# Weight combinations of the down projection: all twelve on GpSimd in the mix stage, tokens loaded earlier, one sample product moved

## The chip, the cores and the metric

The kernel runs on one core of a Trainium2 chip. TensorE (PE) multiplies, VectorE (DVE) and ScalarE (ACT) work on tiles, GpSimd (POOL) does too, SyncE (SP) only issues DMAs; DMAs are issued from the queues of SP, ACT and POOL and run on the same 16 DMA engines. The metric is the time of one execution on the device in microseconds, as the median of the runs shown; lower is better.

## The reference

One step of a decoder layer for 512 prompt tokens and 64 sample tokens (8 sequences of 8). Everything up to the merge of the two attention branches is untouched by the change. What follows it:

```python
br_fox = einsum('btk,kd->btd', o_fox, w_br_fox)      # 512 -> 1024
br_nsa = einsum('btk,kd->btd', o_nsa, w_br_nsa)      # 512 -> 1024
mix = g_fox * br_fox + g_nsa * br_nsa                # gates: sigmoid of 2 x 1024 columns of h @ w_in
x = x + gt1 * einsum('btd,de->bte', mix, w_out)      # 1024 -> 1024
h = rms_norm(x, norm2_g) * (1 + sc2) + sh2
u = relu(einsum('btd,df->btf', h, w_up))             # 1024 -> 4096
y = x + gt2 * einsum('btf,fd->btd', u * u, w_down)   # 4096 -> 1024
```

## The kernel before

A float32 product is made of three passes over halves: each operand is split into a high part (`split`, line 130: an ACT copy, the profile's L113) and a rest (a DVE subtraction, L132), and PE multiplies high by high, low by high and high by low (L78). So every weight tile takes a DMA into a raw tile, an ACT and a DVE instruction before PE can use it. Three raw tiles of 512 KB (`praw`, tag raw) and one more (`pn3`) are shared by all loads of the late stages: a load waits until the split of the tile's last user is done.

The order on each engine is set when the program is built: a scheduler simulates the program and emits each engine's instructions in the order that it finds; a `pin` or `issue_after` keeps an instruction behind a named one in that order. On the chip each engine and each DMA queue takes its instructions strictly in that order.

Four stages matter here.

- **Mix** (`mix_part`). For each of eight column blocks e: two gate products (mg) and two branch products (br) on PE, each with its weights split just before. Beside it POOL makes weight combinations for the down projection. `w_down` is used in a Strassen-like scheme for its rows 0 to 3071: seven products over half matrices in place of eight. Three of these (T1, T2, T3) and T4 need differences of the blocks of w_down. For each k of 0 to 11, two 128-row pieces (one of the upper, one of the lower 1536 rows) are loaded into two tiles td, four subtractions are made in place (`down_sums`), and both tiles are stored to DRAM (tD), from which the late products load them. In the kernel before POOL makes k = 0 to 7 here, with three td tiles, so the loads of the next k wait for a store of the last one.
- **Out** (`out_part`): w_out in four quarters wo0 to wo3. The tiles for wo3's halves lie where the td tiles lay, so wo3's split on ACT waits until the last td store has landed.
- **Up** (`mlp_up`). Pairs n = 3 to 15 of 256 columns, each seven products of 12 matmuls (upNa, upNb, upNe). DVE adds the products from PSUM into a tile u (L101); there are two u tiles. ACT squares u and stores it to DRAM (sD), three DMAs per pair. POOL makes the sums of w_up that a pair needs (L2176). In the kernel before, after pairs 5 and 8 SP loads k = 8, 9 and k = 10, 11 of w_down, 1 MB in each of two DMAs; DVE makes their differences (L1970) in the next iteration, each instruction twice as wide as POOL's; POOL stores them. At the end of the stage `u_load` (in iterations 11, 12, 13) fetches the first two token chunks of sD and splits them (as), and the sample tokens' first block.
- **Down** (`mlp_down`). Products p = 0 to 6 ("11", "21", "T3", ...), each over three chunks c of 512 rows: 24 matmuls dn per chunk on the 256 tokens of a half, with the chunk's weights (wd, 4 places in turn) and tokens (as). For products 0, 1, 4 and 5, each chunk also has a sample part: 8 matmuls dns with sample tokens (sa, or as for the first). In the kernel before, the sample part of chunk c stands right behind chunk c's dn matmuls.

Of the kernel before, what the change touches and what calls it, by code (L numbers as in the profile page):

```python
# [6 lines left out]
F32 = mybir.dt.float32  # L7
# [4 lines left out]
OP = mybir.AluOpType  # L12
AX = mybir.AxisListType

P = 128
D = 1024
# [3 lines left out]
NS = 64  # L20
NT = SEQ + NS
HALF = NT // 2
SQ = 3
# [23 lines left out]
class Step:  # L47
# [1830 lines left out]
    def mix_part(self, pq, pr, mix2):  # L1878
# [49 lines left out]
        def weights(e, x):  # L1928
# [2 lines left out]
                    self.stream(pq, br_src(x, e), [P, 4, P], "wb", f"{x}_{e}", raws=0, parts=1, pin=pin,  # L1931
                                after=None if e else self.first))

        for e in range(NK):
            if e == 0:
                ws = [weights(0, x) for x in range(2)]
                for k in range(8):
                    self.split(oH[:, k], oL[:, k], self.oT[:, k])
                m = [gate(e, x, ws[x][0], True) for x in range(2)]
                for x in range(2):  # L1940
                    branch(e, x, ws[x][1], m[x])
            else:
                m = []
                for x in range(2):
                    mg, br = weights(e, x)
                    m.append(gate(e, x, mg))
                    branch(e, x, br, m[x])
            if e == NK - 1:
                self.wo0 = self.out_weights(0)
            nc.vector.tensor_tensor(m[0], m[0], m[1], op=OP.add)  # L1950
            self.split_pack(mix2[:, e], m[0])
            for k in ((), (0,), (1,), (2, 3), (4,), (5, 6), (7,), ())[e]:
                b = [pq.tile([P, 1, D], F32, tag="td", bufs=3, name=f"td{k}_{i}") for i in range(2)]
                with self.tc.issue_after(self.last_mm):
                    self.down_rows(b, k, "gpsimd")
                    self.down_sums(b, nc.gpsimd)
                    self.down_store(b, k)

    def down_rows(self, b, k, eng):

        n = b[0].shape[1]
        for i in range(2):
            r0 = SQ * 512 * i + P * k
            self.dma(eng, b[i], self.I["w_down"][0, r0:r0 + n * P, :].rearrange("(k p) c -> p k c", p=P))

    def down_sums(self, b, eng):

        (b11, b12), (b21, b22) = [[t[:, :, 512 * h:512 * h + 512] for h in range(2)] for t in b]
        for out, x, y in ((b11, b12, b11), (b12, b22, b12), (b22, b22, b11), (b21, b22, b21)):
            eng.tensor_tensor(out, x, y, op=OP.subtract)  # L1970

    def down_store(self, b, k):

        n = b[0].shape[1]
        for i in range(2):
            self.dma("gpsimd", self.tD[k // 2][:, k % 2:k % 2 + n, i], b[i])

    def gate_prompt(self, pool, j0, scale, uid, **kw):

# [125 lines left out]
        t = pool.tile([P, 4, 2 * NT], F32R, tag=tag, bufs=1, name=f"u2{blk}")  # L2105
        return [t[:, q] for q in range(4)]

    def token_part(self, pool, half, blk, uid, eng="gpsimd", tag="u"):

        t = pool.tile([P, 4, 256], F32, tag=tag, bufs=3, name=f"a{uid}")  # L2110
# [9 lines left out]

    def sample_part(self, pool, tag, blks, room):

        x = pool.tile([P, 4 * len(blks), NS], F32, tag=tag, bufs=3 if tag == "raw" else 1, name=f"sr{blks[0]}_{self.turn}")
# [64 lines left out]
    def mlp_up(self, pu, h3):  # L2188
# [27 lines left out]
        for n in range(FIRST, NP + 1):  # L2216
# [12 lines left out]
                self.tt(o[0][1], b, x, OP.add)  # L2229
            if left:  # L2230
                left()
            if n in (5, 8):
                kd = 8 if n == 5 else 10
                td = self.pb.tile([P, 2, 2, D], F32, tag="x", bufs=1, name=f"td{kd}")
                td = [td[:, i] for i in range(2)]
                self.down_rows(td, kd, "sync")
            if n in (6, 9):
                with self.pinned((self.splits[-1],)):
                    self.down_sums(td, self.nc.vector)
            if n in (7, 10):  # L2240
                self.down_store(td, kd)
            if 0 <= n - NP + 5 < 3:
                self.u_load(n - NP + 5)
            if n == NP:
                break
            product(E, s1, t1, True)
# [6 lines left out]
            def left(n=n, w22=w22, s4=s4, B=B, E=E, b=b, e=e, x=x, u=u, o=o):  # L2253
# [4 lines left out]
                self.act(u, u, AF.Relu)  # L2258
                self.squares_out(n, u)
        self.chain = None  # L2260

    def mlp_down(self, pf):
        nc, I, O = self.nc, self.I, self.O
# [8 lines left out]
        def chunk(key, c):  # L2272

            def src(s):
                if key[0] == "T":
                    v = self.tD[2 * c + s.start // 2][:, :, key in ("T2", "T4")]
                    h = key in ("T2", "T3")
                else:
                    r0, h = 512 * (c + SQ * (key[0] == "2")) + P * s.start, key[1] == "2"
                    v = W[r0:r0 + 256].rearrange("(k p) c -> p k c", p=P)  # L2280
                return [((slice(None),), v[:, :, 512 * h:512 * h + 512])]

            return self.stream(None, src, [P, 4, 512], "wd", f"{key}_{c}", raws=0, room=room(f"wd{key}_{c}", 4))
# [4 lines left out]
        a11 = self.keep.tile([P, SQ, 4, 256], F32, tag="r2", bufs=1, name="a11")  # L2288
        left = [pf.tile([P, 4, 256], F32, tag="late", bufs=3, name=f"s2{c}") for c in range(SQ)]

        def tokens(p, c):

            part = lambda half, blk: self.token_part(pf, half, blk, f"{p}_{half}{blk}")
            if p == 0:
                return part(0, c)
            if p == 1:
                self.dma("gpsimd", a11[:, c], self.sD[c][:, 0:1024].rearrange("p (k t) -> p k t", k=4))
                return part(0, SQ + c)
            if p == 2:
                x, y = part(1, c), part(1, SQ + c)  # L2300
                self.tt(x, a11[:, c], x, sub)
# [13 lines left out]
        sb = None  # L2315
        for p, key in enumerate(("11", "21", "T3", "T2", "T1", "22", "T4")):
# [4 lines left out]
            if sample is not None:  # L2321
                blks = tuple(range(SQ * sample + (p == 0), SQ * sample + SQ))
                xs = self.sample_part(pf, "us", blks, self.ph.tile([P, 4 * len(blks), P], F32R, tag="h3", bufs=2, name=f"sa{p}"))
                xs = xs if p else self.first_sample + xs
            for c in range(SQ):
                w = chunk(key, c)
                if p == 0 and c < 2:
                    a = self.first_parts[c]
                else:
# [2 lines left out]
                for m in range(2):  # L2332
                    n = 0
                    for k in range(4):
                        for x, y in three([t[:, k, P * m:P * m + P] for t in a], [t[:, k] for t in w]):
                            self.mm(pbs[m], x, y, c + n == 0, c == SQ - 1 and n == 11)
                            n += 1
                if sample is not None:
                    for k in range(4):
                        for e in range(2):  # L2340
                            self.mm(sb, xs[c][:, k], w[e][:, k], c + k + e == 0 and p != 5, c == SQ - 1 and k + e == 4 and p != 4)
            for m, pb in enumerate(pbs):
                if p in (0, 2):
                    self.act((c12 if p == 0 else c21)[m], pb)
# [74 lines left out]
    def run(self):  # L2419
        nc, I, O, keep = self.nc, self.I, self.O, self.keep  # L2420
        self.modT = keep.tile([P, 48, 9], F32, name="modT")
        self.gate = keep.tile([P, 5, 24], F32, name="gate")
        self.logf = keep.tile([P, 5, 8], F32, name="logf")
# [4 lines left out]
        self.vc = op.tile([P, NB, P], F32, name="vc")  # L2428
        self.adw = keep.tile([P, 5 * D], F32, tag="r2", bufs=1, name="adw")
        hf = self.adw[:, 0:NK * NT].rearrange("p (k t) -> p k t", k=NK)  # L2430

# [176 lines left out]
```

## Time and profile before

| | us |
|---|---|
| three runs, median (lowest, highest) | 1193.18 (1192.88, 1194.2) |
| the profiled execution's own time | 1192.07 |
| its span, first to last instruction | 1190.4 |
| PE busy in it | 1142.7 |
| DVE, ACT, POOL busy in it | 807.7, 582.4, 249.8 |
| mean granted TensorE clock | 0.991 |

The stages lie in the span at about 586 to 735 (mix), 736 to 790 (out), 790 to 987 (up, the pairs from 830) and 987 to 1190 (down). Rows of the profile name engine, line, operation and tile (output<-inputs, buffer numbers left out); a bracket at a row's end is the idle time just ahead of it on that engine and what ended it. The chain of waits names for each stretch of time what was late there.

### The profile page before, as it was taken

What the parts mean: (1) busy time and instruction counts of PE and PEld (TensorE: products, weight loads), DVE (VectorE), ACT (ScalarE), POOL (GpSimd) and SP (SyncE); (2) the same over time, 40 slices, a digit from 0 to 9 for tenths busy, and PEclk for the clock granted to TensorE, in tenths of its full rate; (3) what the DMA queues carried; (4) which work ended last, traced back from release to release, by engine and by line L of the source; (5) the groups of instructions that cost most, each with busy time, mean ns of one, the idle gap of its engine ahead of it and who ended that gap; (6) DMA issues with size and microseconds to landing.
All of it is one profiled execution on the core that took longest, in us unless ns stands there. A gap on an engine that the chain in (4) does not pass through costs nothing.

```text
span 1190.4 us, 24438 instructions
## 1 busy us (share of the span) xinstructions
PE 1142.7 (96%) x9051; PEld 979.5 (82%) x9051; DVE 807.7 (68%) x1960; ACT 582.4 (49%) x1176; POOL 249.8 (21%) x291
## 2 busy tenths in 40 slices
PE   4999999999999999999999999999997998999998
PEld 3887789999666656777899999889997997888887
DVE  3688785585888856666654444669676754797686
ACT  2455453444776864545532333366544565554520
POOL 2303100000311130000455540003464422110100
PEclk9999999999999999999999999999999999999999
DMA  9897456795785348899998764355755638977632
GB/s 217 206 253 239 154 149 210 251 314 199 228 278 166 108 168 272 294 315 327 229 290 235 231 204 140 109 176 157 240 190 199 225 118 260 332 232 252 215 123 80
DMA packets 187961, 255.46 MB, mean 215 GB/s; under 512 B 22937, under 2 KB 145506, under 8 KB 185666
## 3 DMA queue, kind: packets, MB, share of 16 engines
q1 hardware_dynamic: 148034, 177.22, 48.0%
q0 software_dynamic: 19696, 62.13, 16.2%
q10 hardware_dynamic: 20112, 14.55, 4.4%
q8 instruction: 71, 1.16, 0.4%
q14 instruction: 48, 0.39, 0.1%
HBM read 217.64 MB, written 57.12 MB: 231 GB/s over the span
## 4 chain that ended last, share of the span: by engine, by line
PE 77%; DVE 7%; DMA 7%; ACT 4%; issue 2%; SPq 1%; POOL 1%; ACTq 0%; DVEq 0%; POOLq 0%
PE dn L78 13%; PE mg L78 9%; PE hid L78 7%; PE z L78 6%; PE br L78 4%; PE wo L78 4%; PE up L78 3%; PE ss L78 2%; PE ct L84 2%; PE dns L78 2%; PE so L78 2%; PE k L84 2%; DMA sD<-u 2%; PE ada L78 2%; PE sp L84 1%
## 5 line engine op out<-in xcount | busy, mean ns | idle before, releaser
L78 PE MATMUL z<-winh,h 128*128 128x264 f32 (+1 forms) x576 | 111.1, 286 | 0.3
L78 PEld LDWEIGHTS z<-winh,h 128*128 128x128 f32 x576 | 91.7, 190 | 2.2 <-DVE h L800 0.9
L78 PE MATMUL z<-winl,h 128*128 128x264 f32 (+1 forms) x320 | 88.2, 284 | 0.5 <-DVE winl L132 0.5
L78 PE MATMUL mg<-hH,wml 128*128 128x288 f32 x256 | 75.3, 296 | 0.9 <-DVE wml L132 0.9
L78 PE MATMUL mg<-hH,wmh 128*128 128x288 f32 x256 | 75.3, 296 | 0.0
L113 ACT ACTIVATE xh<-ct 128x256 fp32r<-128x256 f32 x128 | 48.1, 385 | 55.1 <-PE ct L84 30.0
L78 PE MATMUL mg<-hL,wmh 128*128 128x288 f32 x256 | 72.6, 294 | 0.0
L132 DVE TENSOR_TENSOR xl<-ct,xh 128x256 fp32r<-128x256 f32 x128 | 51.7, 420 | 15.1 <-ACT xh L113 13.3
L78 PEld LDWEIGHTS z<-winl,h 128*128 128x128 f32 x320 | 60.6, 190 | 0.7 <-DVE winl L132 0.7
L132 DVE TENSOR_TENSOR wml<-wmr,wmh 128x1024 fp32r<-128x1024 f32 x14 | 19.9, 1419 | 51.2 <-ACT wmh L113 51.2
L78 PEld LDWEIGHTS mg<-hH,wml 128*128 128x128 f32 x256 | 48.1, 188 | 1.1 <-DVE wml L132 1.1
L78 PEld LDWEIGHTS mg<-hH,wmh 128*128 128x128 f32 x256 | 48.1, 188 | 0.2
L78 PEld LDWEIGHTS mg<-hL,wmh 128*128 128x128 f32 x256 | 47.2, 188 | 0.1
L78 PE MATMUL hid<-xh,w1hlk 128*128 128x512 f32 (+1 forms) x160 | 45.1, 370 | 1.5 <-ACT xh L113 1.5
L78 PE MATMUL hid<-xh,w1hlv 128*128 128x512 f32 (+1 forms) x160 | 44.8, 367 | 0.5 <-ACT xh L113 0.5
L132 DVE TENSOR_TENSOR wp<-sums,wp 128x1024 fp32r<-128x1024 f32 x26 | 38.0, 1469 | 7.2 <-ACT wp L113 6.8
L84 PE MATMUL ct<-identF,ro 128*128 128x128 f32 x256 | 36.4, 281 | 5.9 <-DVE ro L116 5.5
L113 ACT ACTIVATE mgt<-mg 128x288 f32<-128x288 f32 x32 | 12.8, 409 | 57.2 <-PE mg L78 57.2
L132 DVE TENSOR_TENSOR wp<-pu,wp 128x512 fp32r<-128x512 f32 (+1 forms) x26 | 30.6, 1181 | 14.8 <-ACT wp L113 14.8
L113 ACT ACTIVATE u<-u 128x1152 f32<-128x1152 f32 x29 | 33.6, 1159 | 10.4 <-DVE u L101 10.1
L78 PE MATMUL br<-oH,wbh 128*128 128x288 f32 x128 | 37.8, 296 | 0.2 <-ACT mgt L113 0.2
L78 PE MATMUL br<-oH,wbl 128*128 128x288 f32 x128 | 37.7, 295 | 0.0
(1181 smaller groups left out, 3709.0 us busy)
## 6 DMA issues: line engine op xcount, KB each, us to landing
adw<-in_w_ada SPq DMA_DIRECT2D x16, 1024.0 KB
foxD<-in_cache_fox_kv SPq DMA_DIRECT2D x128, 128.0 KB
fr<-foxD SPq DMA_DIRECT2D x28, 512.0 KB
sr<-in_cache_nsa_kv SPq DMA_DIRECT2D x112, 128.0 KB
cpg<-in_cache_nsa_kv SPq DMA_DIRECT2D x104, 128.0 KB
pu<-in_w_up SPq DMA_DIRECT2D x26, 512.0 KB
wdr<-in_w_down SPq DMA_DIRECT2D x26, 512.0 KB
wdrT<-tD SPq DMA_DIRECT2D x24, 512.0 KB
```

The lines of the kernel that those rows point to most:

```text
L78: ins = self.nc.tensor.matmul(out, a, b, start=start, stop=stop, skip_group_check=True)
L84: ins = self.nc.tensor.transpose(out, in_, self.identF[:n, :n])
L113: return self.nc.scalar.activation(out, in_, f, **kw)
L132: self.splits.append((eng or self.nc.vector).tensor_tensor(l, x, h.bitcast(F32), op=OP.subtract).ins)
```

## The change

It has five parts.

1. All twelve k are made by POOL in the mix, two per block e from e = 1 on, with four td tiles (two k at a time). The loads of a k stand ahead of the sums of the k before it. To make room, two small tiles (gate, logf) move from one pool to another, which shifts later addresses by 640 bytes.
2. With that, the SP loads, the DVE subtractions and the POOL stores of k = 8 to 11 leave the up stage.
3. `u_load` runs one iteration earlier (10, 11, 12; a fourth call does nothing).
4. The third token chunk of product 0 (`self.third`) is loaded at the end of the up stage into the pn3 tile, and the first one of product 1 (`second`) ahead of the down stage's other token loads; a pin keeps the split of weight chunk ("21", 1) behind the token splits that stand ahead of it.
5. In product 0 the sample parts of chunks 1 and 2 are written behind chunk 2's dn matmuls.

```diff
+        rows = []
         for e in range(NK):
...
-            for k in ((), (0,), (1,), (2, 3), (4,), (5, 6), (7,), ())[e]:
-                b = [pq.tile([P, 1, D], F32, tag="td", bufs=3, name=f"td{k}_{i}") for i in range(2)]
+            for k in ((), (0, 1), (2, 3), (4, 5), (6, 7), (8, 9), (10, 11), (None,))[e]:
                 with self.tc.issue_after(self.last_mm):
-                    self.down_rows(b, k, "gpsimd")
-                    self.down_sums(b, nc.gpsimd)
-                    self.down_store(b, k)
+                    if k is not None:
+                        b = [pq.tile([P, D], F32, tag="td", bufs=4, name=f"td{k}_{i}") for i in range(2)]
+                        self.down_rows(b, k)
+                        rows.append((b, k))
+                    if k is None or k:
+                        self.down_sums(*rows.pop(0))
...
+    def down_rows(self, b, k):
+
         for i in range(2):
             r0 = SQ * 512 * i + P * k
+            self.dma("gpsimd", b[i], self.I["w_down"][0, r0:r0 + P, :])
+
+    def down_sums(self, b, k):
+
+        (b11, b12), (b21, b22) = [[t[:, 512 * h:512 * h + 512] for h in range(2)] for t in b]
         for out, x, y in ((b11, b12, b11), (b12, b22, b12), (b22, b22, b11), (b21, b22, b21)):
+            self.nc.gpsimd.tensor_tensor(out, x, y, op=OP.subtract)
         for i in range(2):
-            self.dma("gpsimd", self.tD[k // 2][:, k % 2:k % 2 + n, i], b[i])
+            self.dma("gpsimd", self.tD[k // 2][:, k % 2, i], b[i])
...
-            if n in (5, 8):
-                kd = 8 if n == 5 else 10
-                td = self.pb.tile([P, 2, 2, D], F32, tag="x", bufs=1, name=f"td{kd}")
-                td = [td[:, i] for i in range(2)]
-                self.down_rows(td, kd, "sync")
-            if n in (6, 9):
-                with self.pinned((self.splits[-1],)):
-                    self.down_sums(td, self.nc.vector)
-            if n in (7, 10):
-                self.down_store(td, kd)
-            if 0 <= n - NP + 5 < 3:
-                self.u_load(n - NP + 5)
+            if 0 <= n - NP + 6 < 4:
+                self.u_load(n - NP + 6)
...
         self.chain = None
+        self.third = self.token_part(self.pn3, 0, 2, "e2", "gpsimd", "raw", 1)
...
-            return self.stream(None, src, [P, 4, 512], "wd", f"{key}_{c}", raws=0, room=room(f"wd{key}_{c}", 4))
+            return self.stream(None, src, [P, 4, 512], "wd", f"{key}_{c}", raws=0, room=room(f"wd{key}_{c}", 4),
+                               pin=(self.splits[-1], self.last_high) if (key, c) == ("21", 1) else None)
...
+        second = self.token_part(pf, 0, SQ, "1_0")
...
             if p == 0:
-                return part(0, c)
+                return self.third
             if p == 1:
                 self.dma("gpsimd", a11[:, c], self.sD[c][:, 0:1024].rearrange("p (k t) -> p k t", k=4))
-                return part(0, SQ + c)
+                return part(0, SQ + c) if c else second
...
+            ws = []
             for c in range(SQ):
                 w = chunk(key, c)
+                ws.append(w)
...
-                if sample is not None:
+                for d in {0: (0,), 1: ()}.get(c, range(1, SQ)) if p == 0 else (c,) if sample is not None else ():
                     for k in range(4):
                         for e in range(2):
-                            self.mm(sb, xs[c][:, k], w[e][:, k], c + k + e == 0 and p != 5, c == SQ - 1 and k + e == 4 and p != 4)
+                            self.mm(sb, xs[d][:, k], ws[d][e][:, k], d + k + e == 0 and p != 5, d == SQ - 1 and k + e == 4 and p != 4)
```

In the mix POOL's queue, with the pieces of k = 1 to 3 (tdK_i is piece i of k in SBUF, tDj the DRAM tile; a DMA td<-in_w_down is a load, tD<-td a store). Before:

```order
L163 DMA td1_0_9830<-in_w_down 128x1024
L163 DMA td1_1_9831<-in_w_down 128x1024
L1970 TENSOR_TENSOR td1_0_9830<-td1_0_9830 128x512
L1970 TENSOR_TENSOR td1_0_9830<-td1_1_9831,td1_0_9830 128x512
L1970 TENSOR_TENSOR td1_1_9831<-td1_1_9831,td1_0_9830 128x512
L163 DMA tD0_9238<-td1_0_9830 128x1024
L1970 TENSOR_TENSOR td1_1_9831<-td1_1_9831 128x512
L163 DMA tD0_9238<-td1_1_9831 128x1024
L163 DMA td2_0_10032<-in_w_down 128x1024
L163 DMA td2_1_10033<-in_w_down 128x1024
```

Of the changed kernel, the same queue:

```order
L1972 TENSOR_TENSOR td2_0_9834<-td2_0_9834 128x512
L1972 TENSOR_TENSOR td2_0_9834<-td2_1_9835,td2_0_9834 128x512
L163 DMA td3_0_9844<-in_w_down 128x1024
L1972 TENSOR_TENSOR td2_1_9835<-td2_1_9835,td2_0_9834 128x512
L163 DMA td3_1_9845<-in_w_down 128x1024
L163 DMA tD1_9239<-td2_0_9834 128x1024
L1972 TENSOR_TENSOR td2_1_9835<-td2_1_9835 128x512
L1972 TENSOR_TENSOR td3_0_9844<-td3_0_9844 128x512
```

The loads of the next k have moved from behind this k's second store to between its subtractions.

On PE at the start of the down stage, from the end of product 0's chunk 1 (dn00 and dn01 are product 0's accumulators, dn10 and dn11 product 1's, dns0 the sample's; wd11_c and wd21_c are weight chunks, as2 the third token chunk, sa0 the sample tokens of blocks 1 and 2; the rows between alternate in the same way). Before:

```order
L78 MATMUL dn01_13472<-wd11_1l_13523,as0_12933 128x512
L78 MATMUL dns0_13473<-wd11_1h_13522,sa0_13474 128x512
L78 MATMUL dns0_13473<-wd11_1l_13523,sa0_13474 128x512
...
L78 MATMUL dns0_13473<-wd11_2h_13564,sa0_13474 128x512
L78 MATMUL dns0_13473<-wd11_2l_13565,sa0_13474 128x512
L78 MATMUL dn00_13471<-wd11_2h_13564,as2_13574 128x512
L78 MATMUL dn01_13472<-wd11_2h_13564,as2_13574 128x512
```

In the changed kernel, at that place:

```order
L78 MATMUL dn01_13498<-wd11_1l_13549,as0_12835 128x512
L78 MATMUL dn00_13497<-wd11_2h_13582,as2_13592 128x512
L78 MATMUL dn01_13498<-wd11_2h_13582,as2_13592 128x512
...
L78 MATMUL dn00_13497<-wd11_2l_13583,as2_13592 128x512
L78 MATMUL dn00_13497<-wd11_2h_13582,as2_13592 128x512 x2
```

And the place to which the sample parts have gone, inside product 1's first chunk:

```order
L78 MATMUL dn11_13639<-wd21_0l_13649,as2_13592 128x512
L78 MATMUL dn11_13639<-wd21_0h_13648,as2_13592 128x512 x2
L78 MATMUL dns0_13499<-wd11_1h_13548,sa0_13500 128x512
L78 MATMUL dns0_13499<-wd11_1l_13549,sa0_13500 128x512
...
L78 MATMUL dns0_13499<-wd11_2h_13582,sa0_13500 128x512
L78 MATMUL dns0_13499<-wd11_2l_13583,sa0_13500 128x512
```

Chunk 2's dn matmuls, which need as2, now follow chunk 1's at once; the sample parts of chunks 1 and 2 come 40 matmuls later than chunk 1's end.

On ACT at the same time (wd21 splits are high halves of product 1's weights, u15 the last pair's square). Before:

```order
L113 ACTIVATE wd21_0h_13624<-wdr21_0_1_13630 128x1024
L113 ACTIVATE u15_13338<-u15_13338 128x1152
L113 ACTIVATE wd21_1h_13671<-wdr21_1_0_13673 128x1024
L163 DMA uD15_11461<-u15_13338 128x1152
L113 ACTIVATE wd21_1h_13671<-wdr21_1_1_13677 128x1024
L113 ACTIVATE sa0_13474<-sr1_157_13475 128x8x64
L113 ACTIVATE as2_13574<-a0_02_13575 128x1024
```

In the changed kernel:

```order
L113 ACTIVATE wd21_0h_13648<-wdr21_0_1_13654 128x1024
L113 ACTIVATE u15_13360<-u15_13360 128x1152
L163 DMA uD15_11501<-u15_13360 128x1152
L113 ACTIVATE as2_13592<-ae2_13484 128x1024
L113 ACTIVATE as2_13592<-a1_0_13495 128x1024
L113 ACTIVATE wd21_1h_13693<-wdr21_1_0_13695 128x1024
L113 ACTIVATE wd21_1h_13693<-wdr21_1_1_13699 128x1024
L113 ACTIVATE sa0_13500<-sr1_157_13501 128x8x64
```

The token split as2 has moved ahead of the two wd21_1 splits and of sa0, but still stands behind wd21_0's second half and the square of u15.

More of the change, by code (lines that the diff above doesn't have):

```diff
@@ L1951, in mix_part @@
             self.split_pack(mix2[:, e], m[0])
-            for k in ((), (0,), (1,), (2, 3), (4,), (5, 6), (7,), ())[e]:
-                b = [pq.tile([P, 1, D], F32, tag="td", bufs=3, name=f"td{k}_{i}") for i in range(2)]
+            for k in ((), (0, 1), (2, 3), (4, 5), (6, 7), (8, 9), (10, 11), (None,))[e]:
                 with self.tc.issue_after(self.last_mm):
-                    self.down_rows(b, k, "gpsimd")
-                    self.down_sums(b, nc.gpsimd)
-                    self.down_store(b, k)
-    def down_rows(self, b, k, eng):
-        n = b[0].shape[1]
+                    if k is not None:
[5 more added lines that the diff above has]
+    def down_rows(self, b, k):
         for i in range(2):
             r0 = SQ * 512 * i + P * k
-            self.dma(eng, b[i], self.I["w_down"][0, r0:r0 + n * P, :].rearrange("(k p) c -> p k c", p=P))
-    def down_sums(self, b, eng):
-        (b11, b12), (b21, b22) = [[t[:, :, 512 * h:512 * h + 512] for h in range(2)] for t in b]
+            self.dma("gpsimd", b[i], self.I["w_down"][0, r0:r0 + P, :])
+    def down_sums(self, b, k):
+        (b11, b12), (b21, b22) = [[t[:, 512 * h:512 * h + 512] for h in range(2)] for t in b]
         for out, x, y in ((b11, b12, b11), (b12, b22, b12), (b22, b22, b11), (b21, b22, b21)):
-            eng.tensor_tensor(out, x, y, op=OP.subtract)
-    def down_store(self, b, k):
-        n = b[0].shape[1]
+            self.nc.gpsimd.tensor_tensor(out, x, y, op=OP.subtract)
         for i in range(2):
-            self.dma("gpsimd", self.tD[k // 2][:, k % 2:k % 2 + n, i], b[i])
+            self.dma("gpsimd", self.tD[k // 2][:, k % 2, i], b[i])
     def gate_prompt(self, pool, j0, scale, uid, **kw):
@@ L2106, in u2_block, with token_part @@
         return [t[:, q] for q in range(4)]
-    def token_part(self, pool, half, blk, uid, eng="gpsimd", tag="u"):
-        t = pool.tile([P, 4, 256], F32, tag=tag, bufs=3, name=f"a{uid}")
+    def token_part(self, pool, half, blk, uid, eng="gpsimd", tag="u", bufs=3):
+        t = pool.tile([P, 4, 256], F32, tag=tag, bufs=bufs, name=f"a{uid}")
         self.dma(eng, t, self.sD[blk][:, 1024 * half:1024 * half + 1024].rearrange("p (k t) -> p k t", k=4))
@@ L2121, in sample_part @@
     def sample_part(self, pool, tag, blks, room):
-        x = pool.tile([P, 4 * len(blks), NS], F32, tag=tag, bufs=3 if tag == "raw" else 1, name=f"sr{blks[0]}_{self.turn}")
+        x = pool.tile([P, 4 * len(blks), NS], F32, tag=tag, bufs=3 if pool is self.praw else 1, name=f"sr{blks[0]}_{self.turn}")
         self.turn += 2
@@ L2421, in run @@
         self.modT = keep.tile([P, 48, 9], F32, name="modT")
-        self.gate = keep.tile([P, 5, 24], F32, name="gate")
-        self.logf = keep.tile([P, 5, 8], F32, name="logf")
         octx = ExitStack()
@@ L2428, in run @@
         self.vc = op.tile([P, NB, P], F32, name="vc")
+        self.gate = op.tile([P, 5, 24], F32, name="gate")
+        self.logf = op.tile([P, 5, 8], F32, name="logf")
         self.adw = keep.tile([P, 5 * D], F32, tag="r2", bufs=1, name="adw")
```

## Prediction

> **What bounds the kernel now.** I read the page's busy line first, then the waits of PE, then busy time by stage, then the chain of waits with the timelines of the engines that it names. The busy line:
>
> ```profile
> PE 1142.7 (96%) x9051; PEld 979.5 (82%) x9051; DVE 807.7 (68%) x1960; ACT 582.4 (49%) x1176; POOL 249.8 (21%) x291
> ```
>
> PE is the bound, and nearly all its instructions stay; so the change can only win back time in which PE waits or runs slowly. The waits of PE in the stages that the change touches (us in total, times, longest):
>
> ```profile
> PE dns L78 <- DVE sa L132: 4.0, 1, 4.0
> PE up8b L78 <- DVE u L101: 3.6, 1, 3.6
> ...
> PE up9b L78 <- DVE u L101: 2.6, 1, 2.6
> ...
> PE up5b L78 <- DVE u L101: 1.3, 1, 1.3
> ...
> PE up6b L78 <- DVE u L101: 0.5, 1, 0.5
> ...
> PE up6e L78 <- DVE u L101: 0.4, 1, 0.4
> ...
> PE up12b L78 <- DVE u L101: 0.3, 1, 0.3
> ```
>
> Six of the seven lie in the up stage; together 8.7 us. The same by stage (start:end, length, busy of PE, PEld, DVE, ACT, POOL, then granted clock, DMA share, GB/s): mix, up's pairs, start of down.
>
> ```profile
> 570.00:735.00 165.00, 163.93 (x1434) 160.23 (x1431) 78.55 (x121) 53.43 (x95) 73.86 (x81) 1.00 0.78 224
> 830.00:985.00 155.00, 146.41 (x1068) 145.00 (x1067) 107.68 (x123) 82.76 (x104) 72.36 (x49) 0.98 0.57 189
> 985.00:1045.00 60.00, 56.03 (x251) 46.62 (x250) 38.40 (x38) 31.66 (x34) 10.56 (x20) 0.94 0.87 301
> ```
>
> PE idles 1.1 us in the whole mix, 8.6 in up (155 − 146.4) and 4.0 at the start of down, and the clock dips in the last two. What the dips cost stands in the chain (start, us, what):
>
> ```profile
> 861.78 1.86 PE up5b L78 x12
> ...
> 889.61 10.26 DMA sD<-u
> 900.50 3.25 PE up8b L78 x12
> 903.75 1.60 PE up9a L78 x12
> ...
> 920.69 3.26 PE up9b L78 x12
> ...
> 1006.89 6.70 PE dns L78 x16
> ...
> 1038.99 1.81 PE dns L78 x8
> ```
>
> Twelve up matmuls take 1.60, but 3.25, 3.26 and 1.86 right behind the three long waits; 16 dns matmuls take 6.70 behind theirs where twice eight at full speed take 3.62.
>
> **Parts 2 and 3: k = 8 to 11 leave up.** Why PE waits there is told by SP's queue and DVE:
>
> ```profile
> 888.72 0.92 SPq L163 DMA_DIRECT2D td<-in_w_down  x2
> ```
>
> ```profile
> 899.99 0.46 DVE L101 TENSOR_TENSOR u<-up8b,sums 128x288 f32<-128x288 f32 x1 [3.83 <-DMA sD<-u]
> ...
> 913.52 2.32 DVE L1970 TENSOR_TENSOR td<-td 128x1024 f32<-128x1024 f32 x1
> ...
> 920.19 0.44 DVE L101 TENSOR_TENSOR u<-up9b,sums 128x288 f32<-128x288 f32 x1
> ...
> 922.66 1.21 DVE L1970 TENSOR_TENSOR td<-td 128x1024 f32<-128x1024 f32 x1
> ```
>
> Two chains end in PE waits. The 2 MB that SP asks for at 888.72 lie beside the square store of 889.61, which takes 10.26 us; DVE's u needs the tile that this store frees, and PE waits 3.6 for up8b. The same is read for up5b. For up9b (and up6b, up6e) DVE itself is late: its wide subtractions, 2.3 us while POOL works too (the last takes 1.21), stand ahead of the u that PE needs. The change removes both the loads and the subtractions. Gain: 8.7 less up12b's 0.3, whose cause is a token load (it stays), is 8.4, and the slow matmuls (3.25 − 1.60) + (3.26 − 1.60) + (1.86 − 1.60) = 3.6: together 12.0; taken from the window's 8.6, 11.9. What is late next is the store without the loads beside it; u_load, moved one iteration ahead, brings its three 0.5 MB token loads beside other stores, where up12b's 0.3 shows the size of such a wait. I put 0.3 on it.
>
> The Trainium skill (TensorE: Matmul & The Clock Gate, Part 1) says that the clock is halved after an idle window of about 3.4 us. The trace agrees for 3.6 and 4.0; it differs for up9b, whose 2.6 us of idle time are followed by half speed (3.26) all the same.
>
> **Part 1: the mix takes over.** One period of POOL's queue for one k, and its first subtraction and last store in the stage:
>
> ```profile
> 592.22 2.55 POOL L1970 TENSOR_TENSOR td<-td 128x512 f32<-128x512 f32 x1 [4.04 <-DMA td<-in_w_down]
> ...
> 677.71 1.06 POOL L163 DMA_DIRECT2D td<-in_w_down  x2
> 683.56 1.29 POOL L1970 TENSOR_TENSOR td<-td 128x512 f32<-128x512 f32 x1 [4.79 <-DMA td<-in_w_down]
> 685.85 3.17 POOL L1970 TENSOR_TENSOR td<-td,td 128x512 f32<-128x512 f32 x2 [1.00 <-DMA td<-in_w_down]
> ...
> 689.56 1.29 POOL L1970 TENSOR_TENSOR td<-td 128x512 f32<-128x512 f32 x1
> 691.15 0.58 POOL L163 DMA_DIRECT2D tD<-td  x1 [0.30 <-POOL td L1970]
> 691.73 0.53 POOL L163 DMA_DIRECT2D td<-in_w_down  x1
> ...
> 704.76 0.58 POOL L163 DMA_DIRECT2D tD<-td  x1 [0.30 <-POOL td L1970]
> ```
>
> ```profile
> td<-in_w_down POOLq DMA_DIRECT2D x16, 512.0 KB, 6.2
> tD<-td POOLq DMA_DIRECT2D x16, 512.0 KB, 4.0
> ```
>
> Before, a k takes 691.73 − 677.71 = 14.0 us: a load wait of 6 stands open in each. The work alone is 1.29 + 3.17 + 1.29 and four issues of 0.55, 8.0. With the loads asked for one k ahead, the second load is issued behind the third subtraction of the k before: from the first issue to its landing 2.1 + 6.2, then one subtraction of 1.5, is about 10; with slower loads and the slow subtractions of the start up to 12.6. I take 11.5. Twelve k then end at 592 + 12 × 11.5 = 730, and the last store lands 4 later, at 734. Who needs it is wo3 on ACT, whose place lies over a td tile:
>
> ```profile
> 741.38 1.05 ACT L113 ACTIVATE wo3h<-wor 128x1024 fp32r<-128x1024 f32 x1
> ```
>
> 734 is 7 us before that. The limit is (741.4 − 4 − 592.2)/12 = 12.1 us for each k. Beside it the mix gets four k more of traffic, 2 MB each: 8 MB on top of 165 us × 224 GB/s = 37 MB, so the DMA share of 0.78 goes towards 0.95. The tightest weights there:
>
> ```profile
> 612.24 1.06 ACT L113 ACTIVATE wmh<-wmr 128x1024 fp32r<-128x1024 f32 x1 [3.28 <-DMA wmr<-in_w_in]
> ```
>
> ```profile
> 620.26 6.38 PE mg L78 x48
> ```
>
> With the DVE rest behind it (1.2) they are ready at 614.5, 5.7 us before PE uses them at 620.3. This cover hides the traffic unless a load comes 5.7 us late. Price: 0 to 5 (a load of 6.2 that takes twice as long, less the cover, comes to 0.5; several such, 5). I take 0.5, since such a load exceeds its cover only once or so.
>
> DVE pays too while POOL subtracts:
>
> ```profile
> 675.71 2.23 DVE L132 TENSOR_TENSOR wml<-wmr,wmh 128x1024 fp32r<-128x1024 f32 x1 [6.31 <-ACT wmh L113]
> ```
>
> Against the 1.21 of an undisturbed instruction of this shape, a split loses 1 us; before its start DVE idles 6.31, so this lies in idle time. The Trainium skill (SBUF — State Buffer, Who interferes with whom) calls the port pair of VectorE and GpSimd an exclusive lock for a whole instruction. The trace agrees (1.21 to 2.3 on DVE). It speaks against this change; what it would do here is a rival below.
>
> **Parts 4 and 5: the start of down.** Before, PE waits 4.0 for sa, whose split stands last in a row on ACT and DVE, behind weight splits that wait for loads. The sample parts now come 40 matmuls later, over 9 us at the 0.226 of a dns at full speed (1.81/8), which covers sa. Gain: 4.0 + (6.70 − 3.62) = 7.1. In their place PE waits for as2 as soon as chunk 1 ends. These rows stand ahead of it:
>
> ```profile
> 1000.78 1.06 ACT L113 ACTIVATE wd_0h<-wdr 128x1024 fp32r<-128x1024 f32 x1 [2.33 <-DMA wdr<-in_w_down]
> 1001.74 1.15 ACT L113 ACTIVATE u<-u 128x1152 f32<-128x1152 f32 x1
> ```
>
> ```profile
> 1002.53 0.39 PE L78 MATMUL dn<-wd_1l,as 128*128 128x512 f32 x1
> ```
>
> Without the two wd21_1 splits and sa, as2's high half would run 1002.8 to 1003.9 and its rest on DVE (1.2) end at 1005.1. PE has its first rest-half matmul at about 1003.1: a wait of up to 2.0; nothing if wd21_0 lands 2 us earlier, for which speaks that two token loads are no longer issued beside it. I take 1.2, bounds 0 and 2.0. On PE the rest of product 0 is queued behind it; ACT and DVE wait for that only with its eviction. The wd21_1 splits come 2.1 us later by the pin; chunk 2 and product 1's first chunk (24 matmuls each, 5.4 us) with 16 dns cover this. And down now starts 12 us sooner against its loads, at a DMA share of 0.87: 0 to 4, and I take 0.3, since up gives up 4 MB of loads and 4 MB of stores just before. The shift of addresses and the smaller tiles cost nothing: no engine works on anything else for it.
>
> **The sum.** Against the profiled execution's 1192.07: −11.9 − 7.1 + 0.3 + 0.5 + 1.2 + 0.3 = −16.7, so 1175.4. The median of the runs lies 1.1 above that execution: 1176.5.
>
> **Rivals.**
>
> *POOL is too slow (slower).* At 14.0 us a k, as now, the last store would land at 592.2 + 12 × 14.0 + 4 = 764, 23 us after wo3's time; PE would stall by that, and the time be 1176.5 + 22.8 = 1199. It decides from 12.1 us a k, and the whole gain is gone from 13.5. For it: the DMA share of 0.78, and the first k's slow subtraction (2.55). Against: the 6 us load wait is just what asking ahead takes away. 0.06, of which 0.04 slower.
>
> *Down is late anyway.* wd21 and the tokens come no sooner though PE does; the 7.1 of down return as other waits, and the 1.2 already counted for as2 is part of them: 1176.5 + 7.1 − 1.2 = 1182.4. For: a share of 0.87 and 301 GB/s there. 0.14.
>
> *Mix weights late* through the DMA share of 0.95: some 4 us, 1180 to 1181. 0.11.
>
> *Lock.* If POOL's 16 more subtractions each block DVE for up to 1.1 us where it is needed, 17.6 us come back: 1194, no change. Against: DVE is busy 78.6 of 165 us and PE idles 1.1 in the mix, though 32 such subtractions are there already. 0.03.
>
> *up9b's slowness is not from its wait,* which is the shortest of those that half speed follows. Then 3.26 − 1.60 = 1.7 stays: 1178.2. Against it: up9a without a wait takes 1.60, and every slow group of the chain has a wait ahead. 0.05. The page of the Trainium skill on the clock, with its 3.4 us, would have it so.
>
> *The waits of up go only partly,* as the stores stay slow beside the w_up loads: half of 11.9 back, 1182.5; all of it, 1188. 0.03.
>
> **How the numbers follow.** The forecast keeps 0.58, with 1174 to 1180 for its own terms. A measurement here tells 0.2%, 2.4 us. Faster: 0.58 + 0.14 + 0.11 + 0.05 + 0.03, and 0.01 of the POOL rival, is 0.92; same 0.03 + 0.01; slower 0.04. Range: at the low end all costs at nothing (−19.0, 1174.2) and 1 more for splits eased elsewhere, 1173; at the high end all at their upper bounds (2.0, 5, 4: 1176.5 + 0.8 + 4.5 + 3.7 = 1185.5), 1186. Lock and POOL lie outside it.
>
> **What would show it.** Right: no wait of PE at up5b, up6b, up6e, up8b, up9b, no L1970 on DVE, twelve matmuls at 1.60 throughout up; POOL at 10 to 12.5 us a k and its last td store landed before wo3's split; mg and br without new waits; no wait at dns, and one of 0 to 2 us at dn on as2 behind chunk 1. Wrong: waits of PE for wo3 or for wml, tokens or wd21 awaited over 3 us in down, or a store sD<-u still at 10 us in up.

## The result, and the profile after

The changed kernel takes 1181.05 us (four runs, 1180.12 to 1181.87) against 1193.03 (four runs) for the kernel before: a ratio of 0.9898, 95% interval 0.9881 to 0.9915, so 12 us faster. The forecast was 1176.5 (1173 to 1186): the direction holds, and 4.5 us of the gain forecast are missing. The profiled execution takes 1180.12 us, its span 1178.5 (before 1192.07 and 1190.4).

The page's busy line of the changed kernel, and the waits of PE from the mix stage on:

```profile
PE 1139.1 (97%) x9051; PEld 973.7 (83%) x9051; DVE 801.9 (68%) x1952; ACT 580.8 (49%) x1176; POOL 272.0 (23%) x319
```

```profile
PE gs L84 <- ACT gp L113: 2.6, 1, 2.6
PE mg L78 <- ACT mgt L113: 0.9, 1, 0.9
PE mg L78 <- DVE wml L132: 0.9, 1, 0.9
PE up3b L78 <- DVE u L101: 0.6, 1, 0.6
PE dn L78 <- DVE as L132: 0.5, 1, 0.5
```

The seven waits shown of before are gone, dns' 4.0 among them; as2 costs 0.5. Three more are new: mg on ACT in the mix; up3b, 0.6, which isn't the change's (e8 below has it too, with the mix and the start of up as before); and gs, eight transposes late in the down stage that the forecast never mentions. The windows of mix, up's pairs and the start of down (columns as before):

```profile
570.00:735.00 165.00, 162.99 (x1371) 159.41 (x1360) 83.05 (x116) 52.33 (x91) 103.75 (x113) 1.00 0.92 277
830.00:973.00 143.00, 142.40 (x1072) 142.17 (x1071) 100.05 (x116) 83.97 (x105) 68.50 (x49) 1.00 0.47 150
973.00:1033.00 60.00, 59.47 (x272) 48.65 (x271) 38.77 (x39) 31.23 (x33) 9.47 (x18) 1.00 0.83 289
```

Up has 0.6 us of idle PE in place of 8.6, and a granted clock of 1.00 throughout. POOL's busy time in the mix rises from 73.9 to 103.8 and the DMA share from 0.78 to 0.92; PE idles 2.0 there in place of 1.1. In the chain of waits up8b and up9b run at full speed, as does the sample part:

```profile
895.08 1.59 PE up8b L78 x12
...
906.24 1.59 PE up9b L78 x12
...
974.79 5.58 PE dn L78 x24
...
1001.61 3.65 PE dns L78 x16
...
1128.32 1.11 PE gs L84 x8
```

But 24 dn take 5.58, at a granted clock of 1.00. In the chain of the kernel before they took 5.44:

```profile
1021.99 5.44 PE dn L78 x24
```

POOL's first subtraction and last store in the mix:

```profile
589.78 2.89 POOL L1972 TENSOR_TENSOR td<-td 128x512 f32<-128x512 f32 x1 [2.38 <-DMA td<-in_w_down]
...
712.57 0.57 POOL L163 DMA_DIRECT2D tD<-td  x1 [0.30 <-POOL td L1972]
```

Twelve k in 123 us are 10.3 each (14.0 before, 11.5 forecast), and the store lands long before wo3's split at 741.

The next table gives the length of each stage on PE, from the timeline, for before, after and every run below: mix (first mg to last br), out (first wo to first up), up (first up3a to first dn), down as far as gp's transposes, from there to gs' transposes, and on to the last dn. It is used more than the medians. Runs of one kernel differ by 1.5 to 8 us, those of before in one set by 12, and in the profiled executions the mix starts anywhere from 573.5 to 577.4, though hardly anything ahead of it is changed; the stage lengths of kernels that share a stage agree within 0.3 us in out and down, and within about 2 in mix and up. A ratio below is about that of the means of the runs, and can differ a little from that of the medians beside it.

| run | mix | out | up | down to gp | gp to gs | to the last dn |
|---|---|---|---|---|---|---|
| before | 159.2 | 57.7 | 155.3 | 146.3 | 7.6 | 45.9 |
| after | 160.6 | 58.5 | 142.8 | 143.4 | 10.3 | 46.1 |
| e1_addr128 | 161.0 | 57.7 | 144.3 | 140.5 | 11.7 | 47.7 |
| e2_before_addr | 159.3 | 58.6 | 155.1 | 149.6 | 7.5 | 46.0 |
| e3_no_down_part | 159.5 | 58.5 | 143.1 | 149.3 | 7.5 | 46.0 |
| e4_down_part_only | 159.0 | 57.7 | 154.6 | 140.5 | 12.3 | 47.3 |
| e5_x2_behind | 161.5 | 58.5 | 142.3 | 143.4 | 6.8 | 46.7 |
| e6_x2_addr | 160.9 | 57.7 | 142.8 | 140.7 | 7.0 | 46.2 |
| e7_no_lookahead | 159.2 | 81.1 | 141.9 | 143.6 | 8.9 | 46.1 |
| e8_up_no_sub | 159.1 | 57.7 | 145.6 | 146.3 | 7.6 | 45.9 |
| e10_late_ahead | 160.0 | 57.7 | 142.8 | 140.6 | 6.8 | 46.1 |
| e11_addr64 | 160.1 | 57.9 | 142.8 | 141.9 | 6.8 | 46.3 |
| e12_gp_first | 161.0 | 58.5 | 142.6 | 143.3 | 7.0 | 46.4 |
| e13_x2_only | 160.6 | 58.5 | 142.7 | 143.5 | 7.5 | 46.0 |

### The profile page after: what moved, and what is told of

It reads as the page before. It is cut to its first block, busy times and chain, and to the rows that moved or that the text cites. A ratio compares the mean times of both kernels' runs of the same rounds, so it can differ in the third digit from the quotient of the medians.

```text
span 1178.5 us, 24445 instructions
## 1 busy us (share of the span) xinstructions
PE 1139.1 (97%) x9051; PEld 973.7 (83%) x9051; DVE 801.9 (68%) x1952; ACT 580.8 (49%) x1176; POOL 272.0 (23%) x319
## 3 DMA queue, kind: packets, MB, share of 16 engines
q1 hardware_dynamic: 146946, 173.03, 47.7%
## 4 chain that ended last, share of the span: by engine, by line
PE 76%; DMA 7%; DVE 6%; issue 5%; ACT 4%; SPq 1%; ACTq 0%; POOL 0%; DVEq 0%; POOLq 0%
PE mg L78 8%; PE dn L78 8%; PE hid L78 7%; PE z L78 7%; PE wo L78 4%; PE br L78 4%; PE up L78 3%; PE ss L78 3%; PE ct L84 2%; PE so L78 2%; PE k L84 2%; DMA ud<-uD 2%; PE ada L78 2%; PE sp L84 1%; DMA winr<-in_w_in 1%
## 5 line engine op out<-in xcount | busy, mean ns | idle before, releaser
L132 DVE TENSOR_TENSOR wp<-pu,wp 128x512 fp32r<-128x512 f32 (+1 forms) x26 | 32.8, 1267 | 16.7 <-ACT wp L113 16.7
(1181 smaller groups left out, 3713.1 us busy)
```

Source lines behind the costliest of these rows:

```text
L132: self.splits.append((eng or self.nc.vector).tensor_tensor(l, x, h.bitcast(F32), op=OP.subtract).ins)
```

## The experiments

**The slow matmuls: addresses.** My theory after the result: the 640 bytes by which part 1 shifts later addresses move the operands that PE loads as stationary ones. By the allocations of the two programs the tokens mix, as and u27 start at 480 modulo 512 before and at 352 after; u26 (used by wd60 and wd61) at 96 before and 480 after; sa, allocated from the other end of the memory, at 480 in both; the streamed weights wo and wd don't move (480 in all of these programs). Two runs change addresses alone. e1 puts them back in the changed kernel:

```diff
         self.adw = keep.tile([P, 5 * D], F32, tag="r2", bufs=1, name="adw")
+        self.room = keep.tile([P, 32], F32, name="room")
```

> The changed kernel with one unused tile of 128 bytes behind the tile adw: the same instructions in the same order, all later left-hand addresses 128 bytes higher, so that the tokens (as, mix, u27) that TensorE loads as stationary operands start again at 480 modulo 512 instead of 352. Address theory: 224 wo, 504 dn and 100 late dn matmuls go from 0.2325 to 0.2267 us apart, 828 x 0.0057 = 4.7 us less, so about 1176.3. Rival (the slow matmuls are a clock or contention effect of that execution, or belong to the new order): nothing changes, 1180.5 to 1181.5, and 24 dn still take 5.58.

e2 shifts them in the kernel before:

```diff
-        self.gate = keep.tile([P, 5, 24], F32, name="gate")
-        self.logf = keep.tile([P, 5, 8], F32, name="logf")
...
         self.vc = op.tile([P, NB, P], F32, name="vc")
+        self.gate = op.tile([P, 5, 24], F32, name="gate")
+        self.logf = op.tile([P, 5, 8], F32, name="logf")
```

> The kernel before with only the two small tiles (gate, logf) moved to the other pool: the same instructions in the same order, later addresses 640 bytes lower. Address theory: wo, dn and wd70/wd71 become slower (828 x 0.0057 = 4.7), wd60/wd61 faster (112 x 0.0057 = 0.6), hid before the mix faster by about 1.5 to 2.0, so 2.1 to 2.6 us slower, 1195.1 to 1195.6, with 24 dn at 5.58 in place of 5.44. Rival (no address effect): 1193.0, 24 dn at 5.44.

Groups of the same shape (count | busy us, mean ns of one, which holds some fixed latency), first in the kernel before, then in e2:

```profile
L78 PE MATMUL dn<-wdT_1h,as 128*128 128x512 f32 x64 | 19.7, 389 | 0.0
...
L78 PE MATMUL dn<-wd60h,u 128*128 128x512 f32 x36 | 11.7, 397 | 0.0
...
L78 PE MATMUL dn<-wd70h,u 128*128 128x512 f32 x32 | 10.2, 389 | 0.0
```

```profile
L78 PE MATMUL dn<-wdT_1h,as 128*128 128x512 f32 x64 | 20.1, 394 | 0.0
...
L78 PE MATMUL dn<-wd60h,u 128*128 128x512 f32 x36 | 11.5, 392 | 0.0
...
L78 PE MATMUL dn<-wd70h,u 128*128 128x512 f32 x32 | 10.4, 395 | 0.0
```

Each group moves the way its address says, wd60 against the others. In the table, out grows by 0.9 and down to gp by 3.3 with the address alone. The time: 1196.2 against 1192.2, ratio 1.0029 (1.0016 to 1.0041), 3.4 us slower. That is more than the 2.1 to 2.6 that I expected, though the interval (1.9 to 4.9 us) holds those too: the gain ahead of the mix for which I had allowed 1.5 to 2.0 doesn't show. e2's mix starts at 575.7, before's at 575.5, and the means of hid<-xl, 512 wide too, go from 397 to 394 ns where the stationary weights move from 96 to 480, and from 395 to 394 where they stay.

In e1 the matmuls are fast again:

```profile
L78 PE MATMUL dn<-wdT_1h,as 128*128 128x512 f32 x64 | 19.9, 389 | 0.0
```

Out returns to 57.7 and down to gp falls by 2.9. Yet the time is 1183.0, ratio 0.9912 (0.9891 to 0.9934), no better than the changed kernel's 0.9898, against my 1176.3. In its profile the end of down gives it back:

```profile
PE gs L84 <- ACT gp L113: 4.0, 1, 4.0
```

From gp to gs 1.4 more than after, and 1.6 more behind it, where the matmuls run slowly at first: 3.0 for the 2.9. What is left of the 2.9 by which this execution is longer than after's lies ahead of the mix (1.7) and in up (1.5), within the spread of the table. So the address effect is real, but a wait at gs swallows what is won ahead of it.

**Which half of the change brings what.** e3 is the changed kernel without parts 4 and 5, e4 the kernel before with these alone. The core of e3 (e4 adds the same lines):

```diff
-        self.third = self.token_part(self.pn3, 0, 2, "e2", "gpsimd", "raw", 1)
...
-        second = self.token_part(pf, 0, SQ, "1_0")
...
-                               pin=(self.splits[-1], self.last_high) if (key, c) == ("21", 1) else None)
...
-                for d in {0: (0,), 1: ()}.get(c, range(1, SQ)) if p == 0 else (c,) if sample is not None else ():
+                if sample is not None:
```

> The changed kernel with the start of the down stage as before: no early third and first token chunk, no pin, sample parts of the first product back behind their chunks. My theory (the two halves of the change are separate): the wait of dns comes back with its slow matmuls, 7.1, against 0.5 + 0.2 for the wait for as2, so 6 to 7 us above the changed kernel, 1187 to 1188; if the 2.6 us wait of gs at the end of down goes with it, 1184 to 1185. Rival (down was late for its loads and its part brought nothing): within 1 us of the changed kernel, 1180 to 1182.

> The kernel before with only the new start of the down stage (parts 4 and 5), k = 8 to 11 still in the up stage, addresses as before. My theory: dns' wait goes, 7.1 less 0.7 for as2 and other small waits: 6 to 6.5 us less, 1186.5 to 1187, 24 dn at 5.44. If the wait of gs at the end belongs to parts 4 and 5, 1189 to 1190 and gs waits 2 to 3 us. Rival (the loads of the start of down were the limit, and only relief in up makes room): the wait returns at another place, 1191 to 1193.

e3: 1186.2, ratio 0.9941 (0.992 to 0.9961), between the two times expected. Up has its full gain without parts 4 and 5 (143.1), dns waits as before, and gs waits no more:

```profile
PE dns L78 <- DVE sa L132: 4.2, 1, 4.2
```

e4's trace shows the other half: down to gp takes 140.5 against 146.3, 5.8 less with the addresses unchanged. And gs waits, for longer still:

```profile
PE gs L84 <- ACT gp L113: 4.5, 1, 4.5
```

So the wait of gs belongs to parts 4 and 5. It isn't PE's being early in the span that makes it: e3 reaches gp 6 us sooner than before and has none. It goes with the length of the stretch from down's start to gp: no wait at 149.3 (e3) and 146.3 (before), 1.2 and 2.6 at 143.6 and 143.4 (e7 and after), 4.0 and 4.5 at 140.5 (e1 and e4). Over the whole of down, gs included, parts 4 and 5 therefore bring 3.0 in the changed kernel (after against e3), and by themselves nothing (e4 against before: 5.8 won, 4.7 lost up to gs and 1.4 behind it). As a time, e4 gave 1193.6, ratio 1.0018 (0.9999 to 1.0036): no gain at all. Its profiled execution was the fastest of its runs (1190.2; they go to 1198.6), 1.9 below before's; what the others lose has no trace and stays open. The median lies by the rival's time, and a wait did return at another place; but that place is gs, not the loads at the start of down, where PE waits 0.5 for as2 as in the changed kernel. The theory stands by the stages, not by this median.

**The wait of gs.** The last two ud loads in the changed kernel are issued by POOL at 1119.25; SP is just issuing the five loads of x2 (2.25 MB, needed only at the very end); on ACT gp's evictions stand behind the split of the ud tile, and PE's gs needs the bank that gp frees. POOL, SP and ACT:

```profile
1119.25 1.06 POOL L163 DMA_DIRECT2D ud<-uD  x2 [12.55 <-DVE u L101]
```

```profile
1118.22 1.75 SPq L163 DMA_DIRECT2D x2b<-x2D  x4
```

```profile
1127.01 0.78 ACT L113 ACTIVATE u<-ud 128x512 fp32r<-128x512 f32 x2 [5.72 <-DMA ud<-uD]
1127.69 1.06 ACT L113 ACTIVATE gp<-gp 128x512 f32<-128x512 f32 x2
```

In the kernel before POOL's first ud load went ahead of x2 (the second came at 1134.06):

```profile
1132.73 0.54 POOL L163 DMA_DIRECT2D ud<-uD  x1 [11.60 <-DVE u L101]
```

```profile
1133.31 2.04 SPq L163 DMA_DIRECT2D x2b<-x2D  x4
```

e5 issues x2's loads on POOL behind the last ud loads, e6 adds the 128 bytes:

```diff
             if not last:
-                x2 = [self.pb.tile([P, 4, D], F32, tag="x", bufs=1, name="x2b")]
...
-                    self.dma("sync", x2[i][:m], self.x2D[:m, i])
...
+            else:
+                x2 = [self.pb.tile([P, 4, D], F32, tag="x", bufs=1, name="x2b")]
...
+                    self.dma("gpsimd", x2[i][:m], self.x2D[:m, i])
```

> The changed kernel with the five loads of x2 (2.25 MB, wanted only at the end) issued by GpSimd behind the last ud loads, in place of SP, which issues them at 1118.2, one us ahead of those. Theory (the wait of gs is the last ud loads' time behind x2's bytes: 7.7 to the landing against 4.8 before): the ud loads land in 4 to 5 us, the wait of gs falls from 2.6 to under 0.5, 2 to 3 us less than the changed kernel, 1178 to 1179. Rival (the wait comes from ScalarE's place in the queue behind the wd splits, not from the landing): gs still waits 2 us or more and the time stays at 1181.

> The run before this one with the unused 128-byte tile as well. Theory (both costs are real, and the faster matmuls of the address run were spent on a longer wait of gs): with the wait gone the 4.7 us of the matmuls count in full, 1173.5 to 1174.5, the fastest of all. Rival (a chain of loads bounds the end of down whatever x2 does): gs or wd waits take its place, 1178 or more.

e5: 1178.4, ratio 0.9873 (0.9848 to 0.9897); e6: 1173.7, 0.9846 (0.9821 to 0.9871), both as the theory had it, and no wait of gs in either. e5's interval overlaps the changed kernel's, e6's doesn't. The landing of the eight ud loads (min, median, max), after and in e5:

```profile
DMA to landing us min/median/max: 3.1/4.9/9.1
```

```profile
DMA to landing us min/median/max: 3.0/4.0/4.5
```

But e5 did two things: the scheduler had also put gp's evictions ahead of that split. e12 does only this, e13 only x2:

```diff
+                if blk == 7 and q == 2:
+                    for i in self.halved:
+                        self.behind(i, self.gated.name)
```

(halved are the two ACT instructions of the third ud split, gated gp's last eviction; e13 is e5 with the opposite order pinned.)

> The run with x2 behind ud had changed two things, as its trace showed: x2's loads, and by the scheduler's choice also the place of gp's two evictions on ScalarE, which stood ahead of the split of the third ud tile and not behind it. Here only the second: the changed kernel, SP loads x2 as in it, gp's evictions ahead of that split. Theory (the order on ScalarE turns the late landing into a wait of TensorE): the ud loads land late as before, 7 to 9 us, but gs waits under 0.3 us, 2.5 to 3 us less than the changed kernel, 1178 to 1178.5. Rival (the landing itself is needed by TensorE at once): the wait moves to the next dn, 1181.

> Here only the first: x2's loads on GpSimd behind the last ud loads, gp's evictions behind the split of the third ud tile as in the changed kernel. Theory (x2's bytes ahead of them make the ud loads late): the last ud loads land in 3 to 5 us after their issue, gs waits 0 to 0.8 us, 1178 to 1179. Rival (the order on ScalarE alone makes the wait): gs waits 2 us or more, 1181.

ACT in e12, then in e13:

```profile
1123.48 1.07 ACT L113 ACTIVATE gp<-gp 128x512 f32<-128x512 f32 x2
1128.49 0.78 ACT L113 ACTIVATE u<-ud 128x512 fp32r<-128x512 f32 x2 [3.94 <-DMA ud<-uD]
```

```profile
1125.36 0.78 ACT L113 ACTIVATE u<-ud 128x512 fp32r<-128x512 f32 x2 [1.15 <-DMA ud<-uD]
1126.04 1.06 ACT L113 ACTIVATE gp<-gp 128x512 f32<-128x512 f32 x2
```

In e12 the landing is as late as in the changed kernel (8.9 at most), and gs doesn't wait; in e13 the order is the old one, the loads are quick (5.6 at most), and gs doesn't wait either (gp to gs 7.0 and 7.5). It takes both, late bytes and the place on ACT; either cure is enough. Their medians, 1180.0 (ratio 0.9892, 0.987 to 0.9914) and 1179.1 (0.989, 0.9865 to 0.9915), are lower than the changed kernel's by 1 to 2 us, which their intervals can't tell from nothing.

**Asking ahead.** e7 takes away the look-ahead and keeps the four tiles:

```diff
-                        rows.append((b, k))
-                    if k is None or k:
-                        self.down_sums(*rows.pop(0))
+                        self.down_sums(b, k)
```

> The changed kernel with each k's loads right ahead of its own subtractions on GpSimd, four td tiles as in it. Theory (asking ahead is what lets twelve k fit in the mix): a k takes 14 us again, the last store lands at 590 + 12 x 14 + 5 = 763, wo3's split and with it TensorE waits some 20 us, 1198 to 1203, slower than before. Rival (wo3 isn't what needs the stores, or four tiles alone are enough): a k takes at most 12 us or wo3 doesn't wait, within 2 us of the changed kernel.

1202.5, ratio 1.0072 (1.0044 to 1.01), slower than before. The last store on POOL, wo3's split on ACT, and the wait of PE:

```profile
761.04 0.58 POOL L163 DMA_DIRECT2D tD<-td  x1 [0.30 <-POOL td L1970]
```

```profile
764.22 2.00 ACT L113 ACTIVATE wo3h<-wor 128x1024 fp32r<-128x1024 f32 x2 [22.58 <-DMA tD<-td]
```

```profile
PE wo L78 <- ACT wo3h L113: 20.7, 1, 20.7
```

With its first subtraction at 591.2 a k takes 14.2. This is the rival that the forecast priced at 1199, with its deadline where it was put; the look-ahead is what keeps the change from it.

**What made up wait.** e8 leaves VectorE's subtractions out of the kernel before:

```diff
-            if n in (6, 9):
-                with self.pinned((self.splits[-1],)):
-                    self.down_sums(td, self.nc.vector)
```

> The kernel before without VectorE's subtractions of k = 8 to 11 in the up stage (these rows of w_down reach the late products as they are loaded; everything else stays, SP's 2 MB loads too). Theory (two causes): the waits of up6b, up6e and up9b go with up9b's slow group, 3.5 + 1.7 = 5.2 us less, and up5b and up8b still wait 1.3 and 3.6, so 1187 to 1188. Rival (the loads alone hold the stage up, VectorE is only the last to come): all waits stay, 1192 to 1193; or (VectorE alone): all go, 1181.

1184.2, ratio 0.9924 (0.9897 to 0.9951), neither value: up5b's wait stays, up8b's goes too. The wait of PE, the chain, and SP's second load of 2 MB in e8; then what SP had waited for in the kernel before:

```profile
PE up5b L78 <- DVE u L101: 1.3, 1, 1.3
```

```profile
889.23 1.60 PE up8b L78 x12
```

```profile
881.56 0.96 SPq L163 DMA_DIRECT2D td<-in_w_down  x2
```

```profile
SPq L163 <- DMA tD<-td: 6.2, 1, 6.2
```

There is one td tile of that size, so the load for k = 10 and 11 had to wait for the store of k = 8 and 9, and that for the subtractions; so it came at 888.72, just ahead of the critical square store, in place of 881.6. The collision was real, but the subtractions had set its hour. Of up's 12 us, 1.3 + 0.3 come from the first load alone and the rest hangs on the subtractions.

**Two more.** e10 starts the look-ahead only at k = 3, e11 is e6 with 64 bytes in place of 128:

```diff
-                    if k is None or k:
+                    if k != 3:
```

> The run with x2 behind ud and the 128-byte tile, and with asking ahead only from k = 3 on: the first three k are loaded, subtracted and stored one after the other as in the kernel before. Theory (the mix takes 1.5 to 2 us longer with twelve k because the first two k's 2 MB and the next ones' come at once at its start, when the weights have the least cover): the mix takes 159.0 to 159.5 again in place of 160.9, the last td store still lands before wo3's split, 1171.5 to 1172.5. Rival (it is the whole traffic at a DMA share of 0.92): the mix keeps its 160.5 to 161.5, 1173.5 to 1174; or the later end on GpSimd makes wo3 wait, above 1175.

> The run with x2 behind ud, the unused tile 64 bytes instead of 128: the stationary operands as, mix and u27 start at 416 modulo 512 (so far 480 went with 0.2267 us, 352 and 96 with 0.2325); sa stays at 480, u26 too. If only 480 is fast: 24 dn at 5.58, dns at 1.81, some 4.7 us more than with 128 bytes, 1178. If addresses that are a multiple of 32 but not of 128 from the slow ones matter in another way: between 5.44 and 5.58, 1174 to 1178.

e10: 1174.7, ratio 0.9855 (0.9834 to 0.9876), a time that wasn't expected either way, and a mix of 160.0, between the two values expected. e3 has the full look-ahead and a mix of 159.5, so one execution differs by more than what was sought: inconclusive. e11: 1178.0, ratio 0.9875 (0.9849 to 0.9902); its chain shows a third speed at 416 modulo 512, beside sa's dns, which stay. The time of its two runs is the one expected of the slow value, but down to gp, at 141.9, lies between the 140.7 of 480 (e6) and the 143.4 of 352 (e5):

```profile
1070.69 1.81 PE dns L78 x8
...
1072.51 5.49 PE dn L78 x24
```

## Why the prediction was right, and where its sizes were off

Stage by stage, on the profiled executions (forecast, measured, from the table):

| | forecast | measured |
|---|---|---|
| ahead of the mix | 0 | −2.0 |
| mix | +0.5 | +1.5 |
| out | 0 | +0.8 |
| up | −11.9 + 0.3 | −12.5 |
| down to gp | −7.1 + 1.2 + 0.3 | −2.9 |
| gp to gs | 0 | +2.7 |
| behind that | 0 | +0.5 |
| sum | −16.7 | −11.9 |

The number lies inside the range in part by luck. It lies outside the 1174 to 1180 that the forecast gave for its own terms, and taken alone it would suit the rival of late mix weights (1180 to 1181); the stages decide against that, since the mix lost only 1.5. The room that the range left for as2, the mix and down's loads was taken by two costs that had been put at nothing.

- *Parts 2 and 3* were right in size, and e3 shows that they need nothing of parts 4 and 5. The reading behind the size was half right: two chains were named, and e8 shows that the second load's collision hung on the other chain.
- *The start of down* was right: with addresses equal it brings 5.8 (e4 against before) and 5.9 (after against e3) as far as gp, for 5.6 forecast; the wait of gs takes back 2.8 of that (after against e3). The wait for as2 is 0.5, inside 0 to 2.0.
- *"The shift of addresses and the smaller tiles cost nothing"* is the step that failed. It costs 0.9 in out and 2.9 to 3.3 in down (e1 and e2), some 4 us in all: I looked for work that it displaces, and not at what an address does to the work that is there.
- *Nothing was put on the end of down*, and this is the second step that failed. PE comes from down's start to gp in 143.4 us in place of 146.3, the last ud loads don't come sooner by as much and meet x2's, and gs lost 2.7. "Down is late anyway" was a rival, but for the loads at its start; the place that became late was one that had some 2 us to spare before (on ACT, gp's first eviction, right behind which gs starts in the changed kernel, ended at about 1138.8, and gs began at 1140.7).
- *The mix* costs 1.5, not 0.5, inside 0 to 5. PE's new wait of 0.9 is on ACT, behind a branch weight that waits for its load (12.2 us in the chain); that mg and br would have no new wait was a sign that didn't come. Executions range from 159.5 to 161.5 with the same look-ahead; whether its start or the whole traffic does it stays open after e10.
- *Ahead of the mix* the 2.0 is this execution's; the starts of the other runs lie on both sides of before's 575.5. Without it the other terms miss by 6.8, not by 4.8.
- *The rivals.* POOL too slow: e7 made it happen, at 1202.5. Lock: DVE's busy time in the mix window rose by 4.5 us, but the only wait of PE on it there is the 0.9 for wml that was there before; it doesn't decide. up9b: its twelve matmuls take 1.59 now that their wait is gone, so their slowness went with it. The Trainium skill (TensorE: Matmul & The Clock Gate, Part 1), with its idle window of about 3.4 us, would have kept it; here the trace decides against it, at 2.6 us. At gs in the changed kernel, 2.6 us too, no half speed followed.
- *The slow matmuls behind up5b* were read as a dip of the clock. The size was right, the reason wasn't: behind a wait of only 0.3, twelve up matmuls took 1.86 too, at a granted clock of 1.00. Behind the waits of 0.6 (up3b, after) and 1.3 (up5b) it is the same 0.26 or 0.27. Before, at up12b:

```profile
956.35 1.86 PE up12b L78 x12
```

## What to carry to other kernels

When PE is the bound, a change that moves a pool also moves its stationary operands: compare their start addresses modulo 512 in both programs before saying that a shift is free, and compare the time of equal groups of matmuls (here 24 dn) afterwards. A stretch of PE's work that gets shorter catches up with loads that used to be ahead of it: list, for its whole length, which waits had only a microsecond or two to spare. Here the two cures, 128 unused bytes and one set of loads issued later, make a version (e6) at 1173.7 that beats both kernels.

## What the runs showed of the hardware

- The spacing of the 128x512 matmuls of wo and dn depends on where the stationary operand starts: 480 modulo 512 gives 5.44 us for 24, 416 gives 5.49, 352 gives 5.58, and 96 goes with the slow value too (wd60 before, 397 ns against 392). e1's operands lie 512 bytes below before's and are as fast. The streamed operand stood still, at 480 modulo 512 too, and the granted clock was 1.00. So whether the start itself counts or its distance from the streamed operand's isn't told apart; why, and whether other starts are faster still, isn't shown either. It isn't a rule for all matmuls: hid<-xl, 512 wide, takes 394 ns both after and in e1, though its stationary operand starts at 480 and at 96. The 288-wide matmuls show no such thing: br's stationary weights moved by the same 640 bytes, and 24 br take 3.18 to 3.19 in both.
- Half speed followed waits of PE of 3.6 and 4.0 us, and in the kernel before one of 2.6 (up9b; the granted clock is 0.59 from 920 to 924), but not the 2.6 of gs in the changed kernel: there the clock is 1.00 throughout. Eight gs transposes took 1.92 behind 4.0 (e1, clock 0.80 from 1123 to 1140), 0.87 without a wait, and 1.11 behind 2.6, which is only the 0.25 that much shorter waits add too (e7's gs takes 1.12 behind 1.2). The windows of before and of the changed kernel:

```profile
920.00:924.00 4.00, 3.31 (x14) 3.31 (x15) 4.00 (x7) 0.03 (x1) 0.68 (x1) 0.59 0.56 217
```

```profile
1124.00:1131.00 7.00, 4.36 (x24) 3.30 (x23) 3.19 (x6) 3.48 (x8) 0.00 (x0) 1.00 0.64 232
```

- 0.58 MB issued one us behind 2.25 MB of another queue landed after 7.7 us and more (9.1 at most), and within 4.5 when issued first (e5).
